# A decoder trunk in which the first MLP product is also made by seven block products, with partial sums copied from bank to bank

## The chip, the cores and the metric

The kernel runs on one core of one Trainium2 chip. Its engines are TensorE (PE, with its weight loads shown as PEld), VectorE (DVE), ScalarE (ACT), GpSimd (POOL) and SyncE (SP), which issues the loads. The metric is the device time in microseconds, as the median of several runs; one further execution was profiled.

## The reference

The reference computes four residual layers over 512 positions of width 1024, all in float32. Each mixer layer is followed by a squared-ReLU MLP with a hidden width of 4096:

```
for layer in range(2):
    h = rmsnorm(x, mix_norm_g[layer])
    x = x + (even_mixer(h) if layer % 2 == 0 else odd_mixer(h))
    h = rmsnorm(x, mlp_norm_g[layer])
    x = x + square(relu(h @ w1[layer])) @ w2[layer]
```

The even mixer is a gated position-mixing MLP beside stick-breaking attention; the odd mixer is a chunked mLSTM. Each ends with an output projection that is added to x.

## The kernel before

Everything stays on the chip: the residual `xs` is held with features on partitions (8 tiles of 128 features x 512 positions), and only weights stream in. Each operand of a float32 product is written as a high part in fp32r and a remainder (`hi`, `lo`), and a product is three matmuls: hi x hi, hi x lo, lo x hi (`mm3`, L289 to L292). So each weight tile of 128 x 1024 is split when it has landed (`w_split`, L185): ScalarE writes the high part (L189), VectorE the remainder (L190; POOL does it for the indices in `POOL_LO`). `stream` (L199) makes these units in order; `w_take` asks for them `LA = 6` units ahead; `NSPL = 5` pairs of split tiles are there. Raw tiles land in two buffers `wr` or, in the second MLP product, in `NRAW = 7` buffers `wq`.

The RMS norm isn't applied to x but folded: the gain goes into the split of x (`split_scaled`, L281), and the reciprocal root, a row over positions (`rrow`), is multiplied in when the hidden layer leaves PSUM (L725).

**At the entry of an MLP** the output projection `w_out` (L321) makes one residual tile after another (L327), and `enter` (L330) splits each of them into `xhi`, `xlo` (L282, L283) and sums its squares (L335 to L339, the sums mostly on POOL).

**The MLP** (`mlp`, L620) goes through the 4096 hidden features in `NG = 4` groups of 1024. A group has two products:

- *The first product* runs over 8 feature tiles. Each is one PSUM bank with 8 x 3 matmuls of 512 columns. VectorE takes it out with relu and the norm (L725), ScalarE squares it (L726).
- *The second product* (`second`, L658) is a 2 x 2 block product done with seven block products in place of eight (the scheme of Strassen and Winograd). Its left blocks are sums of weight blocks: `stream` makes four such sums on VectorE for each set of four weight tiles (`w_sum`, L193 to L196). Its right blocks are sums of hidden blocks: `operands` (L628) makes them from four hidden blocks in each half `q` (splits at L636 and L640, differences at L644 and L654). For each half `s` of the output columns, seven block products of 24 matmuls of 256 columns go into four banks (L674 to L676), and VectorE adds the banks to the residual and to an accumulator `accm` (L686), which is added to the residual in the last group.

PSUM has eight banks, handed out by tag: A 2, B 3, C 2, O 1. The order of the instructions on each engine isn't that of the program text: a planner simulates the program with a cost model, and each engine takes the first instruction in program order that is ready in that simulation. On the chip each engine then runs its own instructions strictly in the planned order, waiting on semaphores. Loads are issued by SP in the same way.

## Time and profile before

| | |
|---|---|
| three runs | 1139.30, 1137.31, 1139.07 us (median 1139.07) |
| the profiled execution | 1138.17 us, its span 1136.4 us |
| granted TensorE clock | 0.994 |
| busy: PE, PEld, DVE, ACT, POOL | 1105.9, 959.9, 825.9, 523.9, 163.9 us |
| loads and stores | 105.18 MB, 93 GB/s on average |

The time is that of the whole launch; the span reaches from the first to the last instruction. A busy PE includes matmuls that overlap: the distance between two starts says how fast they go. Line numbers (L290) are those of the kernel before.

### The profile page before, as it was taken

The page shows a single profiled execution, that of the slowest core. Times are in us where ns is not written, and L with a number is a line of the kernel's source. Part 1 is how long each engine was busy: PE and PEld are TensorE (multiplying, and loading weights), DVE is VectorE, ACT ScalarE, POOL GpSimd, SP SyncE. Part 2 cuts the span into 40 slices and gives each one's busy share as a digit, 9 for nine tenths or more (in the row PEclk, how much of TensorE's full clock was granted, in tenths as well). Part 3 has the DMA queues.
Part 4 walks back from the last instruction along what each step waited for, and adds up shares of the span by engine and source line. Part 5 has one row for each costly group of instructions (what it writes and reads, how often), then busy time and mean ns, then how long its engine had stood idle before and what let it go on. Part 6 is the DMA issues. An engine that isn't in the chain of part 4 may idle for free.

```text
span 1136.4 us, 15912 instructions
## 1 busy us (share of the span) xinstructions
PE 1105.9 (97%) x6372; PEld 959.9 (84%) x6372; DVE 825.9 (73%) x1135; ACT 523.9 (46%) x800; POOL 163.9 (14%) x154
## 2 busy tenths in 40 slices
PE   7899989999999999999999999999999999999998
PEld 5788767878988988988988888887899899899898
DVE  7753599468957957857977677679887677677685
ACT  5343577445435435435555444435543444444441
POOL 7316564540000000000030010003100000000000
PEclk9899999999999999999999999999999999999999
DMA  7222310242241241251042203204324224224121
GB/s 231 92 75 76 105 43 1 74 169 91 94 133 71 97 138 64 93 149 56 20 130 77 93 20 112 93 25 155 118 74 140 83 74 147 76 75 149 37 84 65
DMA packets 34506, 105.18 MB, mean 93 GB/s; under 512 B 3712, under 2 KB 10112, under 8 KB 34432
## 3 DMA queue, kind: packets, MB, share of 16 engines
q1 hardware_dynamic: 34432, 104.17, 28.4%
q8 instruction: 50, 0.82, 0.3%
q14 instruction: 24, 0.20, 0.1%
HBM read 102.06 MB, written 2.10 MB: 92 GB/s over the span
## 4 chain that ended last, share of the span: by engine, by line
PE 79%; DVE 13%; ACT 2%; issue 2%; POOL 2%; DMA 2%; SPq 0%; DVEq 0%; ACTq 0%; POOLq 0%
PE psA L292 10%; PE psA L290 10%; PE psA L291 10%; PE psB L676 7%; PE psB L674 7%; PE psB L675 7%; PE psC L291 5%; PE psC L292 5%; PE psC L290 5%; DVE m L537 2%; DVE wl L190 2%; PE psO L290 2%; PE psO L291 2%; PE psO L292 2%; DVE xlo L283 1%
## 5 line engine op out<-in xcount | busy, mean ns | idle before, releaser
L189 ACT ACTIVATE wh<-wr 128x1024 fp32r<-128x1024 f32 (+1 forms) x124 | 131.3, 1061 | 173.3 <-DMA wr<-wall 53.1
L190 DVE TENSOR_TENSOR wl<-wr,wh 128x1024 fp32r<-128x1024 f32 (+1 forms) x108 | 136.6, 1271 | 84.4 <-ACT wh L189 54.2
L189 ACT ACTIVATE wh<-wq_s 128x1024 fp32r<-128x1024 f32 x64 | 67.2, 1060 | 125.3 <-PE psC L291 57.8
L291 PE MATMUL psA<-xlo,wh 128*128 128x512 f32 x292 | 115.2, 394 | 0.0
L292 PE MATMUL psA<-xhi,wl 128*128 128x512 f32 x288 | 114.1, 396 | 0.5 <-DVE wl L190 0.5
L290 PE MATMUL psA<-xhi,wh 128*128 128x512 f32 x288 | 112.6, 392 | 1.1 <-DVE xres L327 1.1
L291 PE MATMUL psC<-xlo,wh 128*128 128x512 f32 x256 | 102.1, 399 | 0.0
L292 PE MATMUL psC<-xhi,wl 128*128 128x512 f32 x256 | 102.0, 399 | 0.0
L290 PE MATMUL psC<-xhi,wh 128*128 128x512 f32 x256 | 101.2, 395 | 0.0
L292 PE MATMUL psA<-wh,xlo 128*128 128x512 f32 (+2 forms) x232 | 87.7, 380 | 4.0 <-DVE xlo L283 2.2
L290 PE MATMUL psA<-wh,xhi 128*128 128x512 f32 (+2 forms) x232 | 88.4, 383 | 1.8 <-ACT wh L189 1.7
L189 ACT ACTIVATE wh<-wq 128x1024 fp32r<-128x1024 f32 x48 | 50.9, 1060 | 85.2 <-PE psB L675 35.1
L291 PE MATMUL psA<-wl,xhi 128*128 128x512 f32 (+2 forms) x232 | 87.7, 379 | 1.1 <-DVE wl L190 1.1
L190 DVE TENSOR_TENSOR wl<-wq_s,wh 128x1024 fp32r<-128x1024 f32 x64 | 77.5, 1219 | 3.5 <-ACT wh L189 2.5
L339 POOL TENSOR_TENSOR ssq<-ssq,sq 128x512 f32<-128x512 f32 x18 | 28.8, 1600 | 351.8 <-ACT sq L338 351.8
L725 DVE SCALAR_TENSOR_TENSOR r<-psC,rrow 128x512 f32<-128x512 f32 x32 | 22.1, 690 | 60.8 <-PE psC L292 60.8
L290 PEld LDWEIGHTS psA<-xhi,wh 128*128 128x128 f32 x288 | 54.7, 190 | 13.8 <-ACT sq L338 1.5
L291 PEld LDWEIGHTS psA<-xlo,wh 128*128 128x128 f32 x292 | 54.9, 188 | 12.2
L686 DVE TENSOR_TENSOR xres<-xres,psB 128x512 f32<-128x512 f32 x80 | 53.9, 681 | 15.4 <-PE psB L676 14.8
L292 PEld LDWEIGHTS psA<-xhi,wl 128*128 128x128 f32 x288 | 54.1, 188 | 12.2 <-DVE wl L190 0.8
L190 DVE TENSOR_TENSOR wl<-wq,wh 128x1024 fp32r<-128x1024 f32 x48 | 58.6, 1221 | 2.6 <-ACT wh L189 2.3
L290 PEld LDWEIGHTS psC<-xhi,wh 128*128 128x128 f32 x256 | 48.9, 191 | 11.1
(396 smaller groups left out, 3147.4 us busy)
## 6 DMA issues: line engine op xcount, KB each, us to landing
wr<-wall SPq DMA_DIRECT2D x122, 512.0 KB, 3.5
wq<-wall SPq DMA_DIRECT2D x64, 512.0 KB, 3.9
out<-xres SPq DMA_DIRECT2D x16, 128.0 KB, 1.8
wr<-wv SPq DMA_DIRECT2D x2, 528.0 KB, 3.5
xres<-xT SPq DMA_DIRECT2D x4, 256.0 KB, 5.7
xres<-xT SPq DMA_DIRECT2D x2, 512.0 KB, 8.6
lngb<-lngb SPq DMA_DIRECT2D x1, 512.0 KB, 5.4
sgr<-sgw SPq DMA_DIRECT2D x1, 512.0 KB, 6.2
```

What stands on the lines that cost most here:

```text
L189: act.activation(hi[:, :n], raw, AF.Copy)
L190: (gp if i in POOL_LO else dve).tensor_tensor(lo[:, :n], raw, f(hi[:, :n]), op=ALU.subtract)
L290: pe.matmul(out, lhsT=lh, rhs=rh, start=first, stop=False)
L291: pe.matmul(out, lhsT=lh, rhs=rl, start=False, stop=False)
L292: pe.matmul(out, lhsT=ll, rhs=rh, start=False, stop=last)
L339: (dve if i == KT - 1 else gp).tensor_tensor(ssq, ssq, j, op=ALU.add)
L537: dve.tensor_tensor_scan(m[:, ::-1], m[:, ::-1], ones.to_broadcast([P, n]), 1.0, op0=ALU.mult, op1=ALU.mult)
L674: pe.matmul(o, lhsT=lh, rhs=rh, start=first, stop=False, skip_group_check=True)
L675: pe.matmul(o, lhsT=lh, rhs=rl, start=False, stop=False, skip_group_check=True)
L676: pe.matmul(o, lhsT=ll, rhs=rh, start=False, stop=fin, skip_group_check=True)
L686: add = lambda dst, b, op=ALU.add: dve.tensor_tensor(dst, dst, b, op=op)
L725: dve.scalar_tensor_tensor(r, b, 0.0, rb[0], op0=ALU.max, op1=ALU.mult)
```

## The change

The first product is also made by seven block products. Its blocks are the four quarters of x (features 0 to 511 and 512 to 1023, positions 0 to 255 and 256 to 511) and those of the weights of a group. Hidden features are now made in two quarters `q` of seven products each, with 256 columns in a matmul.

The same function `product` serves both products. A bank is no longer added up on VectorE into an accumulator: after a11, ScalarE copies the bank, negated, into a second one, a12 goes on in the first, s2 in the second; after s2 ScalarE copies the second into a third, where n3 and a22 go on. So that matmuls add to what ScalarE wrote, an identity product is made into these two banks once at the start of each MLP. In the first product ScalarE also copies n1's bank to SBUF.

Both products read weights in sets of four tiles. Of the four sums of a set, VectorE makes two (`c`, and `b21` in place), and two are made by loads that add to what stands in the buffer (`w_acc`, issued by POOL). So b12 and b22 are each loaded twice. The raw buffers `wq` are 5 for 7.

At the entry the operands of the first product are made: the projection's tiles come in the order 0, 4, 1, 5, 2, 6, 3, 7, and for each pair ScalarE scales, VectorE makes one difference and three more, and seven blocks are split. The relu and square follow each block as it is finished, and the hidden blocks' sums are made from them as before. Pools are placed and opened at other points: the weights' and the sums' pools lie on the right side and are opened before the entry.

```diff
+            b11 = w_load(i, True)
+            w_split(b11, i)
+            yield
+            b = w_load(i + 1, True)
+            w_acc(b, i + 2)
+            b21 = w_load(i + 3, True)
+            w_split(b21, i)
+            yield
+            c = wpool.tile([P, 1056], F32, name=f"wc{i}", tag="wr", bufs=2)[:, :1024]
+            dve.tensor_tensor(c, b, b11, op=ALU.add)
+            w_split(c, i)
+            yield
+            dve.tensor_tensor(b21, c, b21, op=ALU.add)
+            w_acc(b11, i + 1)
+            w_split(b11, i)
+            yield
+            w_split(b, i)
+            yield
+            w_split(w_load(i + 2), i)
+            yield
+            w_split(b21, i)
...
+    def w_acc(t, i):
+        gp.dma_start(out=t, in_=wall[i if i < V0 else i - 2], accum_op=ALU.add)
...
+    def operands_of(ep, kept):
+        def operand(norm, d):
+            g, k = pc(f"g{norm}", d), d % 4
+            if d < 4:
+                t = ep.tile([P, 3, H], F32, name=f"xa{norm}_{d}", tag="xa", bufs=2)
+                act.activation(t[:, 1:], xs[:, d, :].rearrange("p (e t) -> p e t", e=2), AF.Copy, scale=g)
+                dve.tensor_tensor(t[:, 0], t[:, 1], t[:, 2], op=ALU.subtract)
+                split(e1[0][:, k, 0:2], e1[1][:, k, 0:2], t[:, 0:2])
+                kept[k] = t
+            else:
+                x = ep.tile([P, 2, H], F32, name=f"xb{norm}_{d}", tag="xb", bufs=1)
+                act.activation(x, xs[:, d, :].rearrange("p (e t) -> p e t", e=2), AF.Copy, scale=g)
+                split(e1[0][:, k, 2:4], e1[1][:, k, 2:4], x)
+                t = ep.tile([P, 3, H], F32, name=f"xc{norm}_{d}", tag="xc", bufs=1)
+                dve.tensor_tensor(t[:, 0], kept[k][:, 2], x[:, 1], op=ALU.subtract)
+                dve.tensor_tensor(t[:, 1], kept[k][:, 1], t[:, 0], op=ALU.subtract)
+                dve.tensor_tensor(t[:, 2], x[:, 0], t[:, 1], op=ALU.subtract)
+                split(e2[0][0][:, k], e2[0][1][:, k], t)
...
+            for tag in "CB":
+                pe.matmul(bank(tag, 0), lhsT=identb, rhs=identb.unsqueeze(1).to_broadcast([P, 4, P]), start=True, stop=True)
+            def product(ops, copy=None):
+                ws = dict(zip(PROD, w_take(7)))
...
+                ba, bd, bx, bc = bank("A"), bank("C", 0), bank("B", 0), bank("O")
+                prod("a11", ba, True, False)
+                act.activation(bd, ba, AF.Copy, scale=-1.0)
+                prod("a12", ba, False, True)
+                yield 0, 0, two(ba), None, None
+                prod("s2", bd, False, False)
+                act.activation(bx, bd, AF.Copy, scale=-1.0)
+                prod("n1", bc, True, True)
+                prod("n3", bx, False, False)
+                pc5 = two(bc)
+                if copy is not None:
+                    act.activation(copy, pc5, AF.Copy)
+                    pc5 = copy
+                yield 1, 1, pc5, two(bx), ALU.subtract
+                prod("n4", bd, False, True)
+                yield 0, 1, pc5, two(bd), ALU.add
+                prod("a22", bx, False, True)
+                yield 1, 0, two(bx), None, None
+            def first(q, ops):
...
+                for tb, fb, b, b2, op in product(xop, tmp("p", "ad", AD)):
+                    t = h[tb, fb] = tmp(f"h{tb}{fb}", "h", HB)
+                    if b2 is not None:
+                        dve.tensor_tensor(t, b, b2, op=op)
+                        b = t
+                    rv = rb[0][:, tb * H:(tb + 1) * H].unsqueeze(1).to_broadcast([P, 2, H])
+                    dve.scalar_tensor_tensor(t, b, 0.0, rv, op0=ALU.max, op1=ALU.mult)
+                    act.activation(t, t, AF.Square)
+                    if (tb, fb) != (1, 0):
+                        put(f"a{tb + 1}{fb + 1}", t)
+                n1 = diff("n1", h[1, 0], h[1, 1])
+                s2 = tmp("s2", "ad", AD)
+                dve.tensor_tensor(s2, h[0, 0], n1, op=ALU.subtract)
+                put("s2", s2)
+                diff("n3", h[0, 0], h[1, 0])
+                diff("n4", h[0, 1], s2)
             def second(g, ops):
                 for s in range(2):
+                    for tb, nb, b, b2, op in product(ops):
+                        x = blk(nb, tb, s)
+                        dve.tensor_tensor(x, x, b, op=ALU.add)
+                        if b2 is not None:
+                            dve.tensor_tensor(x, x, b2, op=op)
...
-        r = enter(w_out(w_take(2), y_of(3), "AAO"), 3, ssq)
+        with tc.tile_pool(name="xe", bufs=1, side="right") as ep:
+            r = enter(w_out(w_take(2), y_of(3), "AABB", HALVES), 3, ssq, operands_of(ep, {}))
```

221 lines of the change are left out of this document (87 added, 134 removed).

## The prediction

> **What bounds the kernel now.** I read the page's busy times first, then the windows over the MLP stages, then the chain of waits, then the two places where a new MLP begins.
>
> ```profile
> span 1136.4 us, 15912 instructions
> PE 1105.9 (97%) x6372; PEld 959.9 (84%) x6372; DVE 825.9 (73%) x1135; ACT 523.9 (46%) x800; POOL 163.9 (14%) x154
> PE 79%; DVE 13%; ACT 2%; issue 2%; POOL 2%; DMA 2%; SPq 0%; DVEq 0%; ACTq 0%; POOLq 0%
> ```
> ```profile
> 221.30:246.00 24.70, 22.83 (x102) 17.96 (x101) 20.67 (x22) 15.96 (x22) 13.89 (x9) 1.00 0.29 97
> 781.00:806.00 25.00, 23.67 (x104) 18.23 (x103) 24.92 (x27) 14.14 (x20) 10.45 (x8) 1.00 0.50 168
> ```
> ```profile
> 560.00:600.00 40.00, 37.73 (x311) 36.62 (x311) 30.61 (x39) 24.53 (x36) 11.73 (x16) 1.00 0.30 94
> ...
> 860.00:960.00 100.00, 100.00 (x658) 91.57 (x657) 76.36 (x90) 40.98 (x49) 0.00 (x0) 1.00 0.35 115
> 960.00:1060.00 100.00, 100.00 (x609) 89.41 (x608) 70.21 (x84) 41.65 (x51) 0.00 (x0) 1.00 0.34 106
> ```
>
> After the window come its length and the busy time of PE, PEld, DVE, ACT and POOL. Inside an MLP (860 to 1060) PE has no gap at all, at a granted clock of 1.00: what is taken from PE there is taken from the time, as long as the others keep up. VectorE is next, with 70 to 76 us in 100. At the two entries, where the output projection hands the residual to an MLP (221 to 246, 781 to 806), VectorE is nearly full already, 20.67 us in 24.70 and 24.92 in 25.00, and PE stays busy there only because it can start on the first product one input tile at a time.
>
> **The matmul saving.** PE starts in one layer group of MLP 0: first wide matmul of a stretch, first narrow one, first wide one of the next group.
>
> ```profile
> 410.50 0.39 PE L290 MATMUL psC<-xhi,wh 128*128 128x512 f32 x1
> ...
> 449.36 0.28 PE L674 MATMUL psB<-a11h,wh 128*128 128x256 f32 x1
> ```
> ```profile
> 494.89 0.39 PE L290 MATMUL psC<-xhi,wh 128*128 128x512 f32 x1
> ```
>
> From 410.50 to 449.36 PE issues seven feature tiles of 24 wide matmuls, 168: 38.86 / 168 = 0.2313 us each. From 449.36 to 494.89 it issues the 336 narrow ones of the second product (2 halves x 7 products x 24) and one wide tile of 24: (45.53 - 24 x 0.2313) / 336 = 0.1190 us. The first product is 192 wide now, 44.4 us, and becomes 2 quarters x 7 x 24 = 336 narrow, 40.0 us. That is 4.4 us in a group and **35.4 us in eight groups** (4 in each of 2 MLPs). A narrow matmul might have been held up by its weight load; the second product shows that it isn't, as its 0.119 us hold both.
>
> **VectorE's load in a group.** Durations of rows overlap by a start-up; the cost in a queue is the distance between starts:
>
> ```profile
> 376.00 0.68 DVE L686 TENSOR_TENSOR xres<-xres,psB 128x512 f32<-128x512 f32 x1
> 376.60 1.22 DVE L190 TENSOR_TENSOR wl<-wq,wh 128x1024 fp32r<-128x1024 f32 x1
> 377.74 0.69 DVE L640 TENSOR_TENSOR n4l<-n,n4h 128x512 fp32r<-128x512 f32 x1
> 378.34 1.22 DVE L196 TENSOR_TENSOR wq_s<-wq_s,wq 128x1024 f32<-128x1024 f32 x1
> ```
>
> So 0.60 us for 512 columns and 1.14 us for 1024. Now: 8 + 14 weight remainders and 8 weight sums (30 x 1.14 = 34.2), 8 relu steps, 22 operand steps, 14 residual adds (44 x 0.60 = 26.4): 60.6 us in 84.4. After: 28 remainders and 2 sums for each of 4 sets (36 x 1.14 = 41.0; the other two sums of a set go to the loads), in each quarter 4 relu steps, 2 subtractions out of a bank and 11 operand steps (34 x 0.60 = 20.4), 12 residual adds (7.2): 68.6 us in 80.0. It fits over the group. It doesn't fit over the first product alone: there 18 x 1.14 + 20.4 = 40.9 us stand against 40.0 of PE. What carries it over is the lead: five pairs of split weights (NSPL) let VectorE be up to five remainders, 5.7 us, ahead. I take no loss in the six groups that follow another group; the bound on the other side is the first rival below.
>
> ScalarE has room: 28 weight splits, 2 x (3 bank copies, 4 squares, 7 splits) and 2 x 2 bank copies are 28 x 1.06 + 32 x 0.63 = 49.8 us in 80.
>
> ```profile
> L189 ACT ACTIVATE wh<-wq_s 128x1024 fp32r<-128x1024 f32 x27 | 28.3, 1060 | 55.5 <-PE psC L291 28.2 <-PE psO L675 16.0 <-PE psB L675 7.2
> ...
> L726 ACT ACTIVATE h<-r 128x512 f32<-128x512 f32 x31 | 19.4, 625 | 6.3 <-DVE r L725 6.2
> ```
>
> **The copy between banks.** Each product begins with a11, then ScalarE copies the bank (negated) to a second one, and only then may a12 go on in the first: PE ends its last matmul 0.28 - 0.12 = 0.16 us after it could start another, the copy is as long as the 512-column row above, 0.63, and two hand-offs add about 0.03 each (the relu step started at 337.33, where the last matmul of its bank ended, 336.90 + 0.40): 0.85 us. This copy is free where n1, which goes to a bank of its own, is there to fill it: the trace shows that the order is planned so (n4 of one group stands between two wide matmuls at 494.54 and 494.66, in the midst of the next group's first tile). n1 is 24 x 0.119 = 2.86 us, enough for this gap and for the second copy after s2. It isn't there at the step from the first to the second product of a group, since its operand needs the last hidden block, which PE finished just one product earlier. I take one open gap in each group, **8 x 0.85 = 6.8 us**; bounds 0 and all four in a group, 27.
>
> ```profile
> 336.90 0.40 PE L292 MATMUL psA<-xhi,wl 128*128 128x512 f32 x1
> ```
> ```profile
> 337.33 0.69 DVE L725 SCALAR_TENSOR_TENSOR r<-psA,rrow 128x512 f32<-128x512 f32 x1 [1.42 <-PE psA L292]
> 494.54 0.28 PE L676 MATMUL psB<-n4h,wl 128*128 128x256 f32 x1
> 494.66 0.39 PE L292 MATMUL psA<-xhi,wl 128*128 128x512 f32 x1
> ```
>
> **The two entries.** Here a gain is given back. Now a residual tile needs one remainder on VectorE; after, a pair of tiles needs a difference (256 columns), two remainders of 512, three differences of 256 in a row and a remainder of 768.
>
> ```profile
> 204.69 0.42 DVE L287 TENSOR_TENSOR atl<-psC,ath 128x256 fp32r<-128x256 f32 x1
> ```
>
> With 0.34 us for 256 columns (0.42 less the same 0.08 overlap) and 0.87 for 768 (between 0.60 and 1.14), a pair costs 4 x 0.34 + 2 x 0.60 + 0.87 = 3.43 us against 2 x 0.66 now; four pairs +8.4 us. What counts for PE is when the last tile that a11 needs is split:
>
> ```profile
> L283 DVE SCALAR_TENSOR_TENSOR xlo<-xres,par,xhi 128x512 fp32r<-128x512 f32 x8 | 10.5, 1367 | 0.0
> ```
> ```profile
> 235.23 2.44 DVE L283 SCALAR_TENSOR_TENSOR xlo<-xres,par,xhi 128x512 fp32r<-128x512 f32 x2
> 796.30 2.44 DVE L283 SCALAR_TENSOR_TENSOR xlo<-xres,par,xhi 128x512 fp32r<-128x512 f32 x2
> ```
> ```profile
> 230.57 0.40 PE L290 MATMUL psA<-xhi,wh 128*128 128x512 f32 x1
> 235.36 0.51 PE L292 MATMUL psA<-xhi,wl 128*128 128x512 f32 x1 [0.46 <-DVE wl L190]
> 244.00 1.02 PE L266 MATMUL psC<-onesd,ssq 128*128 128x1 f32 x8 [1.41 <-DVE ssq L339]
> 789.89 0.40 PE L292 MATMUL psA<-yoh,wl 128*128 128x512 f32 x1
> 791.39 0.47 PE L290 MATMUL psA<-xhi,wh 128*128 128x512 f32 x1 [1.11 <-DVE xres L327]
> ```
>
> At the even entry the last remainder ends at 237.67. All but the last pair's second half (2.5 us) of the 8.4 comes before a11's last input: 243.6. Nine of a11's matmuls (1.07 us) can run ahead, so PE stands as if it had begun at 242.5, where now it begins at 230.57 and loses 0.46 + 1.41: **10.1 us lost**. At the odd entry 798.74 + 5.9 - 1.07 = 803.6 against PE's being free at 790.12, where now it loses 1.27: **12.2 us lost**. Bounds for both together: 5 if splits of weights now in front of them move behind, 36 if the first product behind each also runs at VectorE's pace (7 us more each, by rival 1 without a lead).
>
> The first set of MLP 0 has an index in POOL_LO, and in the new loop all seven remainders take that index: seven go to POOL, at
>
> ```profile
> L190 POOL TENSOR_TENSOR wl<-wr,wh 128x1024 fp32r<-128x1024 f32 x16 | 38.7, 2428 | 9.0 <-ACT wh L189 8.9
> L339 POOL TENSOR_TENSOR ssq<-ssq,sq 128x512 f32<-128x512 f32 x18 | 28.8, 1600 | 351.8 <-ACT sq L338 351.8
> ```
>
> 17.0 us. That takes 7 x 1.14 = 8.0 us off VectorE, but VectorE's remainders beside POOL's sums at the entry took 1367 ns against 690 alone (377.74 above): 8 x 0.68 = 5.4 us lost beside six sums of 1600 ns on POOL, 9.6 us, so 17.0 us would cost 9.6. I take nothing; bounds -8 and +9.6. The Trainium skill, "SBUF — State Buffer", section "Who interferes with whom", states this as a rule: a VectorE instruction with two SBUF inputs contends with a GpSimd instruction that reads SBUF. By that rule the offload is worth nothing, as the row says; without it the sum would be 8 us lower.
>
> **What else moves.** The last group of an MLP makes 12 residual adds for 20 now (8 x 0.60 = 4.8 us), where PE idles 2.3 us between 560 and 600; I take **-2**. The cleared accumulator on POOL stood beside PE's work and gives nothing. The pools' new places and the order of the projection's tiles only decide when loads may start.
>
> The two sums made by loads: b12 += b22 and b11 += b12, issued by POOL, whose queue in the MLP holds nothing else. No accumulating load is in this trace. The nearest rows:
>
> ```profile
> wr<-wall SPq DMA_DIRECT2D x122, 512.0 KB, 3.5
> wq<-wall SPq DMA_DIRECT2D x64, 512.0 KB, 3.9
> ```
> ```profile
> q1 hardware_dynamic: 34432, 104.17, 28.4%
> ```
>
> Loads rise by 64 x 0.52 MB, to some 38% of the queues' time. The sum b12 + b22 is made a set ahead and hidden. b11 + b12 is not: it may start when b11's remainder and the sum c are done, and n1's split waits for it, at the head of ScalarE's queue, with the bank copies behind it. With five pairs b11's remainder is done about 9.1 us before a11 starts, and n1's split may start 2.9 us before: 6.2 us for the load. Bounds: 3.5 us (a plain load, hidden) and 7.0 (read and add one after the other); I take the first end's side, hidden, because nothing but the add is new. By the Trainium skill, "DMA: Bandwidth & Descriptors", section "Anatomy of one DMA — SWDGE (gpsimd) path", a load on this path takes 2.0 us and its bytes at 436 GB/s, an estimate of 3.2 us, which would also be hidden; no run here shows it.
>
> **Sum:** -35.4 + 10.1 + 12.2 + 6.8 - 2 = -8.3 us. The profiled execution took 1138.17 us (span 1136.4), so 1129.9; the median of the runs lies 0.9 above it: **1131 us**.
>
> **Rivals.** (1) *VectorE becomes the bound of the first product*, slower. For: 40.9 us against 40.0, and VectorE now idles much in front of the relu steps, since the order of its queue is fixed:
>
> ```profile
> L725 DVE SCALAR_TENSOR_TENSOR r<-psC,rrow 128x512 f32<-128x512 f32 x4 | 2.8, 691 | 9.3 <-PE psC L292 9.3
> L725 DVE SCALAR_TENSOR_TENSOR r<-psA,rrow 128x512 f32<-128x512 f32 x4 | 2.8, 690 | 2.9 <-PE psA L292 2.9
> ```
>
> These 12.2 us are one group's. If half stays and half the lead is used up, the first product takes 40.9 + 6.1 - 2.9 = 44.1 us, 4.1 over PE, in six groups 24.6: **1155 us**. It decides from 1.4 us a group. Against: the second product needs only 27.7 us of VectorE in 40.0 and can refill the lead. (2) *The accumulating load is late*, slower: 7.0 us against 6.2, 0.8 us in each of 32 sets, 26 us: **1156 us**; it decides from 0.26 us a set. Against: slots may be free earlier than I reckon. (3) *The entries stay hidden*, faster: 5 us for both and the gaps filled, 1139.07 - 35.4 + 5 - 2 = **1107 us**. For: VectorE waits for PE before the even entry, and work may be moved there; against: 24.92 of 25.00 at the odd one.
>
> ```profile
> 221.35 1.29 DVE L327 TENSOR_TENSOR xres<-psA,xres 128x512 f32<-128x512 f32 x2 [9.55 <-PE psA L292]
> ```
>
> (4) *The change doesn't do what it says*: the planned order finds something else, all gains are eaten, about **1139 us**.
>
> **Chances.** Forecast 0.40 (its own range 1118 to 1142), (1) 0.20, (2) 0.10, (3) 0.22, (4) 0.08. A measurement of this kernel can tell about 0.2% (2.3 us) from no change. Of the forecast's 0.40, 0.33 is faster, 0.03 the same, 0.04 slower; (3) is faster throughout; of (1) and (2) 0.27 is slower, 0.01 the same, 0.02 faster; of (4) 0.04, 0.02, 0.02. Faster 0.61, same 0.06, slower 0.33. The range, 1105 to 1155, reaches into (3) and (1) and leaves 0.2 out.
>
> **What will show it.** Right: PE in the MLP in narrow matmuls 0.119 us apart and groups of 80 to 82 us; a PE gap of 8 to 15 us at each entry, released by VectorE's or ScalarE's work on the new sums; gaps of about 0.85 us released by ScalarE's bank copy, once a group; VectorE at 85% in the MLP. Wrong: gaps in the first product released by VectorE's remainders in every group (1); ScalarE's split idle for an accumulating load (2); no gap at the entries (3); groups near 84 us.

## The result and the profile after

The changed kernel is slower: 1222.09 us (median of 4 runs, 1219.65 to 1227.29) against 1138.19 us for the kernel before (median of 4, 1134.69 to 1139.30). The ratio is 1.0749, with a 95% interval of 1.0701 to 1.0796. The forecast was 1131 us, with a range of 1105 to 1155: the sign was wrong, and the time lies far outside the range. The profiled execution took 1219.65 us.

The head of the page after, with its busy times, the clock in 40 slices, POOL's DMA queue (packets, MB, share of 16 engines' span) and the shares of the chain of waits:

```profile
span 1217.9 us, 18697 instructions
PE 1104.1 (91%) x7528; PEld 1004.7 (82%) x7528; DVE 911.5 (75%) x1222; ACT 627.9 (52%) x954; POOL 223.5 (18%) x221
PEclk8999999869999999999999999997899999999999
q0 software_dynamic: 9216, 33.56, 15.6%
PE 41%; DMA 24%; DVE 22%; ACT 6%; issue 5%; POOL 3%; SPq 1%; POOLq 0%; ACTq 0%; DVEq 0%
```

Before, the chain was 79% PE and 2% DMA; now PE has 41% and DMA 24%. Apart from the first slice the clock drops at the two entries (slices 8 and 9, and 28 and 29 of the 40). The windows over the two entries and two times 100 us of the second MLP (length, busy time of PE, PEld, DVE, ACT and POOL, clock, DMA share, GB/s), first the kernel before at its even entry, then the changed kernel:

```profile
200.00:260.00 60.00, 58.13 (x255) 46.72 (x254) 33.96 (x41) 29.63 (x42) 28.18 (x15) 0.97 0.39 132
```
```profile
200.00:260.00 60.00, 40.72 (x174) 31.98 (x172) 41.25 (x46) 29.80 (x45) 35.72 (x20) 0.82 0.37 105
800.00:860.00 60.00, 49.15 (x224) 39.95 (x223) 52.71 (x90) 31.49 (x59) 13.39 (x12) 0.82 0.17 45
860.00:960.00 100.00, 92.17 (x744) 89.50 (x744) 74.57 (x86) 51.26 (x67) 7.80 (x9) 0.99 0.53 137
960.00:1060.00 100.00, 92.84 (x763) 90.45 (x761) 77.84 (x90) 49.69 (x65) 8.80 (x10) 1.00 0.55 137
```

Two things show at once. At the even entry PE is busy for 40.72 of 60 us, where it was busy for 58.13. And inside the MLP, where PE had no gap, it has 7 to 8 us of gaps in 100, while VectorE is hardly fuller than before (74.57 and 77.84 against 76.36 and 70.21). The chain of waits inside the MLP says what PE waits for, in the end (start, length, what). Line numbers from here on are those of the changed kernel: L197 is ScalarE's split, L198 VectorE's remainder, L203 the adding load.

```profile
864.61 1.24 DVE wl L198
865.86 4.26 DMA wq<-wall
870.16 0.59 issue
870.77 0.64 POOL wq L203
871.41 7.40 DMA wq<-wall
878.89 1.07 ACT wh L197
879.99 1.23 DVE wl L198
...
887.65 4.22 DMA wq<-wall
...
893.46 7.40 DMA wq<-wall
900.94 1.07 ACT wh L197
```

This is one turn in a set of weights, and it comes again 22 us later. A remainder of VectorE sets a raw buffer free (865.86). Only then the plain load of the next set's b12 begins (4.26 us). When it has landed, POOL issues the two adding loads, back to back, the next set's b12 + b22 and this set's b11 + b12. The first lands 5.3 us after its issue. The second, issued 0.64 us behind it in the same queue, takes 7.40 us, and ScalarE has stood idle for it, in front of the split of n1's weights. So the loop is raw buffer, load, adding load, split, remainder, raw buffer. The loads of the MLP by who issues them, with the median from issue to landing:

```profile
wq<-wall SPq DMA_DIRECT2D x96, 512.0 KB, 3.6
wr<-wall SPq DMA_DIRECT2D x90, 512.0 KB, 4.0
wq<-wall POOLq DMA_DIRECT2D x64, 512.0 KB, 5.6
```

The 5.6 us mix two kinds. By the landing times in the trace, 34 of the 64 adding loads were issued when the one before had landed, and took 5.4 us at the median; the other 30 were issued while the one before was still under way, and took 7.25.

**A measure for the stages.** A set is the 168 narrow matmuls of seven products; at 0.119 us each that is 20.0 us. An MLP has four groups of four sets: two of the first product (q0, q1), two of the second (s0, s1). From the starts of its matmuls, the time of each set of the changed kernel is, in us:

| | group 1: q0 q1 s0 s1 | group 2 | group 3 | group 4 | sum |
|---|---|---|---|---|---|
| MLP 0 | 49.0 24.9 23.8 20.0 | 21.1 24.9 24.0 20.2 | 21.1 23.1 24.0 20.4 | 21.3 23.2 23.9 23.6 | 388.3 |
| MLP 1 | 40.8 23.1 24.0 22.3 | 21.2 23.1 24.4 20.2 | 21.0 23.7 24.1 20.3 | 20.9 23.5 24.1 20.8 | 377.6 |

Both MLPs take 765.9 us, where 32 dense sets would take 640. The rest of the launch takes 1219.65 - 765.9 = 453.8 us. Nearly all the experiments below have 453 to 460 us for that rest, too, so they are compared by their MLPs. The kernel before, from the first wide matmul of an MLP to its last narrow one, takes 346.6 and 340.9 us, 687.5 for its two. Nearly all the experiments are single runs, each good to some 8 us (the changed kernel's four took 1219.65 to 1227.29, the kernel before 1134 to 1140 beside these runs). They are set against the profiled execution of the changed kernel, the fastest of its four; the sets agree better than that.

### The profile page after: what moved, and what is told of

The parts are those of the page before. It is cut to its first block, busy times and chain, and to the rows that moved or that the text cites. A ratio compares the mean times of both kernels' runs of the same rounds, so it can differ in the third digit from the quotient of the medians.

```text
span 1217.9 us, 18697 instructions
## 1 busy us (share of the span) xinstructions
PE 1104.1 (91%) x7528; PEld 1004.7 (82%) x7528; DVE 911.5 (75%) x1222; ACT 627.9 (52%) x954; POOL 223.5 (18%) x221
## 3 DMA queue, kind: packets, MB, share of 16 engines
q0 software_dynamic: 9216, 33.56, 15.6%
## 4 chain that ended last, share of the span: by engine, by line
PE 41%; DMA 24%; DVE 22%; ACT 6%; issue 5%; POOL 3%; SPq 1%; POOLq 0%; ACTq 0%; DVEq 0%
DMA wq<-wall 22%; DVE wl L198 7%; PE psA L298 5%; PE psA L300 5%; PE psA L299 5%; ACT wh L197 3%; PE psB L697 2%; PE psO L300 2%; PE psO L298 2%; PE psA L698 2%; PE psO L299 2%; PE psA L697 2%; DVE m L588 2%; PE psA L699 2%; PE psB L698 2%
## 5 line engine op out<-in xcount | busy, mean ns | idle before, releaser
L197 ACT ACTIVATE wh<-wq 128x1024 fp32r<-128x1024 f32 x160 | 168.2, 1056 | 220.3 <-DMA wq<-wall 97.6
L198 DVE TENSOR_TENSOR wl<-wq,wh 128x1024 fp32r<-128x1024 f32 x155 | 190.6, 1231 | 72.3 <-ACT wh L197 72.1
L203 POOL DMA_DIRECT2D wq<-wall x64 | 56.6, 964 | 610.0 <-DMA wq<-wall 282.3
L197 ACT ACTIVATE wh<-wr 128x1024 fp32r<-128x1024 f32 (+1 forms) x92 | 97.2, 1058 | 57.1 <-DMA wr<-wall 32.7
L198 DVE TENSOR_TENSOR wl<-wr,wh 128x1024 fp32r<-128x1024 f32 (+1 forms) x77 | 97.4, 1269 | 36.3 <-ACT wh L197 33.4
L698 PE MATMUL psA<-xlo,wh 128*128 128x256 f32 x256 | 76.9, 300 | 10.4 <-DVE xlo L295 10.3
L697 PE MATMUL psA<-xhi,wh 128*128 128x256 f32 x256 | 77.0, 301 | 4.4 <-ACT psC L704 4.2
L697 PE MATMUL psB<-xhi,wh 128*128 128x256 f32 x256 | 73.0, 285 | 4.6 <-ACT psB L708 4.6
L699 PE MATMUL psA<-xhi,wl 128*128 128x256 f32 x256 | 75.6, 295 | 0.0
L699 PE MATMUL psB<-xhi,wl 128*128 128x256 f32 x256 | 72.1, 282 | 0.0
L698 PE MATMUL psB<-xlo,wh 128*128 128x256 f32 x256 | 72.0, 281 | 0.0
L697 PE MATMUL psC<-e2h,wh 128*128 128x256 f32 x256 | 71.3, 279 | 0.0
L698 PE MATMUL psC<-e2l,wh 128*128 128x256 f32 x256 | 71.1, 278 | 0.0
L197 ACT ACTIVATE wh<-wc 128x1024 fp32r<-128x1024 f32 x32 | 33.9, 1060 | 38.5 <-PE psB L698 30.7
```

What stands on the lines that cost most here:

```text
L197: act.activation(hi[:, :n], raw, AF.Copy)
L198: (gp if i in POOL_LO else dve).tensor_tensor(lo[:, :n], raw, f(hi[:, :n]), op=ALU.subtract)
L203: gp.dma_start(out=t, in_=wall[i if i < V0 else i - 2], accum_op=ALU.add)
L697: pe.matmul(o, lhsT=lh, rhs=rh, start=first, stop=False, skip_group_check=True)
L698: pe.matmul(o, lhsT=lh, rhs=rl, start=False, stop=False, skip_group_check=True)
L699: pe.matmul(o, lhsT=ll, rhs=rh, start=False, stop=fin, skip_group_check=True)
```

## The experiments

All the kernels are the changed one with the edit shown, if nothing else is said. Where an instruction is left out, the planner makes a new order, which can cost or give some us by itself.

### The adding loads

In the first kernel the two adding loads of a set are left out; in the second they are plain loads into the same buffers. In both the sums b12 + b22 and b11 + b12 are missing from the result.

```diff
 e1_no_acc
-        gp.dma_start(out=t, in_=wall[i if i < V0 else i - 2], accum_op=ALU.add)
+        pass
 e2_plain_load
-        gp.dma_start(out=t, in_=wall[i if i < V0 else i - 2], accum_op=ALU.add)
+        gp.dma_start(out=t, in_=wall[i if i < V0 else i - 2])
```

> The changed kernel without its 64 accumulating loads: the two weight sums of a set that they make are left out (b12 and b11 go on as they landed); splits, VectorE's two sums, copies and matmuls all stay. The changed kernel's profiled execution took 1219.65 us: 81.5 more than before = -35.4 (matmuls) + some 44 (PE's standstill at the two entries, less what it was before) + some 73 over eight groups. Theory A (the wait for accumulating loads, with the raw buffers behind them, makes the 73): most of it goes, 1150 to 1165. Rival B (VectorE, with 68.6 us of work in a group of 80 and an order that is fixed, makes it): no more than 15 us go, 1205 or more. Rival C (the bank copies on ScalarE make it): as B.

> The changed kernel with the same 64 loads from POOL's queue as plain loads, without the add: they overwrite (so two sums of a set are left out), and every wait, buffer and byte stays. If it is the add that makes these loads slow (5.6 us from issue to landing against 3.6 for the others): landing falls to about 4 and the time by 20 to 50 us. If it is the chain itself (slot free, load, issue from POOL, load again, sum, split): less than 15 us go, 1205 to 1220.

Without the loads: 1189.07 us, between what the two theories expected; this kernel has a new planned order, and its s0 sets take 24.3 us where plain loads leave 23.2, so its time isn't the price of the loads alone. With plain loads: 1175.49 us, and this kernel has the same planned order as the changed one on every engine, the same bytes and the same number of loads. So 1219.65 - 1175.49 = **44.2 us are the price of the add alone**, 46.3 in the MLPs (719.6 for 765.9). Its page and its loads:

```profile
q0 software_dynamic: 9216, 33.56, 8.4%
```
```profile
wq<-wall POOLq DMA_DIRECT2D x64, 512.0 KB, 4.2
```

For the same 33.56 MB the queue's share is 8.4% where it was 15.6%, and a load lands in 4.2 us where it took 5.6 (3.8 for 5.4 when the one before had landed, 4.5 for 7.25 when it was still under way). The difference of the medians is 1.4 us, and 64 of them would be 90 us if they all counted; half of it does. By position in a group (mean of groups 2 to 4, both MLPs; s1 without the last group), the sets take:

| | q0 | q1 | s0 | s1 |
|---|---|---|---|---|
| changed kernel | 21.1 | 23.6 | 24.1 | 20.3 |
| plain loads | 19.7 | 21.0 | 23.2 | 20.0 |

The adds cost some 5.2 us in a group, most of it in the first product, where VectorE has most to do by the prediction's count.

**The kernel before with adding loads** in its second product, with its seven raw buffers:

```diff
 e4_before_acc (the kernel before)
-                b12 = w_load(i + 1, True)
-                b22 = w_load(i + 2, True)
-                b = w_sum(b12, b22)
+                b = w_load(i + 1, True)
+                w_acc(b, i + 2)
...
-                w_split(w_sum(b11, b12), i)
+                w_acc(b11, i + 1)
+                w_split(b11, i)
```

> The kernel before with one part of the change alone: in the second product b12+b22 and b11+b12 are made by accumulating loads from POOL in place of VectorE (7 raw buffers as before, 16 sets in place of 32). Theory A in its strong form (the load's own time is what costs): 16 sets x 2.3 us = 35 us, 1165 to 1180. Weak form (the load costs only where raw buffers are few, 5 in the change): 1137 to 1145, since here 7 buffers serve sets that are needed half as often.

1148.23 us against 1140.1 for the kernel before on the same chip: 8.1 us for 16 sets, 0.5 us a set, though VectorE is spared 32 sums. That lies between the two forms of the theory, just above the weak one, and it is a difference of two single runs. An adding load lands in 5.4 us here, and each was issued when the one before had landed:

```profile
wq<-wall POOLq DMA_DIRECT2D x32, 512.0 KB, 5.4
```

So the operation is as slow where everything else is as before. With two raw buffers more, and a set needed half as often, it costs a third as much in a set (46.3 / 32 = 1.4 us).

**A sixth raw buffer**, for b21 of every second set (room is made by four hidden buffers for five, and by smaller constants):

```diff
 e5_six_raw
-            b21 = w_load(i + 3, True)
+            b21 = w_load(i + 3, True, (i - m) % 8 == 4)
...
+            raw = mpool[0].tile([P, 1024], F32, name=f"wx{i}", tag="wx", bufs=1)
```

> The changed kernel with a sixth raw buffer (b21 of every second set has one of its own; one hidden-block buffer fewer makes the room), so that two sets can be in the buffers at once: b12 of the next set can land, and take its accumulating load, while the present set is in use. e2 showed that 44 us go when the same loads don't add, in the same order of every engine. Theory A1 (the add is late because the loads start late, when a buffer comes free): 15 to 40 us go, 1180 to 1205. Rival A2 (the add is late because of its own length, wherever it starts: the planned order leaves it about 4 us and it takes 5.6): less than 10 us go, 1210 to 1222.

1193.33 us, 26 us less, with adding loads that land no sooner (6.1 us). The sets q0 and q1 come down to 20.1 and 21.1, nearly as with plain loads, and the MLPs take 737.7 us, 28 of the 46.3 less. So more than half of what the adds cost comes from the lack of raw buffers: the chain of loads starts too late to hide.

**All four sums on VectorE**, with b22 loaded once:

```diff
 e6_dve_sums
-            w_acc(b, i + 2)
+            b22 = w_load(i + 2)
+            dve.tensor_tensor(b, b, b22, op=ALU.add)
...
-            w_acc(b11, i + 1)
+            dve.tensor_tensor(b11, c, b22, op=ALU.subtract)
```

> One part of the change undone: no accumulating loads, all four sums of a set on VectorE (b += b22, c = b + b11, b21 += c, b11 = c - b22), b22 landing once in the two other raw buffers. VectorE's load rises from 68.6 to 77.7 us in a group of 80. If VectorE has the room: about what e2 took, 1165 to 1185. If VectorE is the bound (rival B): 5 us and more in a group on top of e2, 1215 and more.

1231.40 us, 12 more than with adding loads. In the MLP VectorE then has 87.71 us in 100:

```profile
960.00:1060.00 100.00, 94.17 (x766) 92.99 (x765) 87.71 (x99) 52.81 (x68) 0.00 (x0) 0.97 0.31 102
```

The first product isn't what gets longer: in the later groups q0 takes 19.7 and q1 22.5 us, less than in the changed kernel, but s0 takes 27.0 for 24.1, and the rest of the launch 462 for 454. So all four sums on VectorE are no cheaper than the adding loads. That VectorE couldn't have made them in time isn't shown apart, since b22 here also holds one of the two buffers that the sum c uses.

**The order of the adding loads.** POOL's planned queue has, for three sets in four, the next set's first adding load ahead of this set's second one, which is n1's. This edit queues the second one ahead:

```diff
 e18_add_order
+        with (ExitStack() if b11 or last[0] is None else tc.issue_after(last[0])):
+            ins = gp.dma_start(out=t, in_=wall[i if i < V0 else i - 2], accum_op=ALU.add)
+        if b11:
+            last[0] = ins.ins
```

> The whole computation. In the changed kernel POOL's queue has, for three sets in four, the next set's first adding load (b12 + b22) ahead of this set's second one (b11 + b12, n1's weights); the first waits for a plain load into a raw buffer that comes free late. Here the second one is queued ahead. Theory (n1's weights are late because their load stands behind the other one in POOL's queue): they come some us earlier in each set, and half or more of the 46 us of the adding loads is had back, 1180 to 1200. Rival (the raw buffers set the pace, and what one load gains the other loses, since the next set's sum b then comes later): 1210 to 1235.

1232.66 us, 13 more: the rival holds. What POOL waits for is another thing now, a remainder of VectorE in place of a load that has to land. First the changed kernel, then this one:

```profile
POOL wq L203 <- DMA wq<-wall: 282.3, 20, 24.4
POOL wq L203 <- DVE wl L198: 172.2, 10, 24.2
```
```profile
POOL wq L206 <- DVE wl L198: 545.7, 28, 27.0
POOL wq L206 <- DMA wq<-wall: 63.0, 11, 24.3
```

q0 and q1 take 20.8 and 23.4 us, a little less than before, but s0 takes 26.3 for 24.1. So this other order doesn't help. It fits the waits that what n1 gains, the next set's b loses, for want of time between a raw buffer's release and its next use.

### The step to the second product

With plain loads s0 still takes 23.2 us. PE's rows in one such set of that kernel, at its two gaps, and ScalarE's at the same time:

```profile
961.32 0.28 PE L699 MATMUL psO<-n1h,wl 128*128 128x256 f32 x1
963.03 0.38 PE L697 MATMUL psA<-a12h,wh 128*128 128x256 f32 x1 [1.42 <-ACT psC L704]
...
971.07 0.28 PE L698 MATMUL psA<-a11l,wh 128*128 128x256 f32 x1
972.63 0.38 PE L697 MATMUL psB<-n3h,wh 128*128 128x256 f32 x1 [1.28 <-ACT psB L708]
```
```profile
959.97 1.06 ACT L197 ACTIVATE wh<-wq 128x1024 fp32r<-128x1024 f32 x1 [1.79 <-PE psB L698]
960.93 0.62 ACT L744 ACTIVATE h<-h 128x512 f32<-128x512 f32 x1
961.45 1.04 ACT L197 ACTIVATE wh<-wr 128x1024 fp32r<-128x1024 f32 x1
962.40 0.58 ACT L704 ACTIVATE psC<-psA 128x512 f32<-128x512 f32 x1
...
964.99 0.64 ACT L294 ACTIVATE n1h<-n 128x512 fp32r<-128x512 f32 x1 [0.94 <-DVE n L733]
...
971.03 1.06 ACT L197 ACTIVATE wh<-wq 128x1024 fp32r<-128x1024 f32 x1 [0.94 <-PE psC L698]
971.99 0.58 ACT L708 ACTIVATE psB<-psC 128x512 f32<-128x512 f32 x1
```

Both gaps end with a bank copy (L704, L708), and the copy stands in ScalarE's queue behind a split of weights that had to wait for PE (at 959.97 and 971.03). From start to start PE loses 1.71 - 0.12 and 1.56 - 0.12, 3.0 us together. Three kernels ask whether that is the copies, VectorE's load, or the operands that come late. All three have plain loads (two sums left out). In addition, the first has no copies from bank to bank: s2 and n3 begin their banks anew, so the partial sums are not carried on. The copy of n1's bank to SBUF stays.

```diff
 e7_no_copies
-                act.activation(bd, ba, AF.Copy, scale=-1.0)
...
-                prod("s2", bd, False, False)
-                act.activation(bx, bd, AF.Copy, scale=-1.0)
+                prod("s2", bd, True, False)
...
-                prod("n3", bx, False, False)
+                prod("n3", bx, True, False)
```

> e2 (plain loads) without ScalarE's two bank copies in each product: the second and third bank begin with their own first matmul, so the sums lack the products that the copies carry over. Against e2's 1175.49. If PE's wait for the copies makes the 29 us that e2 leaves in the groups: 1145 to 1157. If it is hidden but for one gap in each group, as predicted (6.8 us): 1165 to 1172. If nothing: within 4 us.

1186.25 us, 11 more, which none of the three expectations had. In a new planned order q1 takes 19.6 us for 21.0 and s0 26.7 for 23.2. Where the copies stood, PE now waits (860 to 1170 us) for the copy of n1's bank to SBUF (L711), for the subtraction ahead of relu (L738) and for an operand (L294):

```profile
PE psO L697 <- ACT p L711: 6.8, 3, 5.1
PE psB L697 <- DVE h L738: 4.8, 3, 1.6
PE psA L697 <- ACT a12h L294: 3.8, 3, 1.3
```

So the copies account for some of q1's gap, but leaving them out doesn't close the gap in s0; as the order is new, it doesn't show more than that. The next two take nearly the same off VectorE in a first product, 4.6 and 4.8 us, but only the second shortens the way from the last hidden block to the operands. The first leaves out both weight sums of VectorE as well; the second leaves out the four differences of hidden blocks and splits the blocks themselves.

```diff
 e11_no_sums
-            dve.tensor_tensor(c, b, b11, op=ALU.add)
-            w_split(c, i)
+            w_split(b, i)
...
-            dve.tensor_tensor(b21, c, b21, op=ALU.add)
 e12_no_chain
-                    dve.tensor_tensor(d, a, b, op=ALU.subtract)
-                    put(n, d)
-                    return d
+                    put(n, a)
+                    return a
...
-                dve.tensor_tensor(s2, h[0, 0], n1, op=ALU.subtract)
+                s2 = h[0, 0]
```

> Left out: the adding in the loads, and both weight sums that VectorE makes in a set (b12 and b21 as loaded are split in their place). This takes 2 x 1.14 us of VectorE from each set, 36 to 34 operations of the weights being left. Theory (VectorE is the bound of the first product, 40.9 us against 40.0, and its lateness shows in the first set of the second product, 23.2 us for 20): at 36.3 against 40.0 the second and third sets of a group come down to 20 to 21 us, 8 x 3 to 4 us less, about 1148. Rival (the chain of hidden operands behind the last block, not VectorE's load): the third set stays at 23, 1168 to 1176.

> Left out: the adding in the loads, and the four differences of hidden blocks in each quarter; the blocks themselves are split in their place, so that no operand waits for another. This takes 8 x 0.6 = 4.8 us off VectorE in a first product, as much as the two weight sums are in its two sets (4.6). Theory of VectorE's load: as much as without the weight sums, about 1148. Rival (the chain n1, s2, n4 behind the last block sets it): third set 20 to 21 for 23.2, 1150 too, while the run without weight sums gains nothing; if neither gains, the cause is in neither.

Without the sums s0 takes 22.6 us for 23.2, and 1164.57 us in all: 10 less in the MLPs, about half of it in s0. The first set of MLP 0 shrinks by 4.8 us, that of MLP 1 grows by 2.8. Without the differences s0 takes **20.0 us in every one of the six later groups**, and 1149.70 us in all; the MLPs take 693.1 for 719.6, 26.5 less. With as much taken off VectorE in both, it is the chain n1, s2, n4 behind the last hidden block that makes the gap, and hardly VectorE's load.

The chain can also be gone around: a22 needs only a block that is there early. In this kernel it is made third in s0, in a bank of its own.

```diff
 e15_a22_early
-                ws = dict(zip(PROD, w_take(7)))
+                ws = dict(zip(("a11", "a12", "a22", "s2", "n1", "n3", "n4") if early else PROD, w_take(7)))
...
+                if early:
+                    by = bank("B", 2)
+                    prod("a22", by, True, True)
                 prod("s2", bd, False, False)
```

> The whole computation. In the first half of each second product, a22 (whose operand is there early) is made third, in a bank of its own, ahead of s2, n1, n3, n4, which wait for the chain of hidden operands; its weights come third too; VectorE adds one bank more to the residual. Theory (the chain leaves PE idle for 3.2 us in a group): a22's 2.9 us fill the gap, 8 x 2.5 to 3 us less than 1222, about 1199; n1's weights, made by the adding load, get 2.9 us more, which can give some us more. Rival (the adding loads decide there too, and PE only waits one product later): 1215 to 1225.

1209.79 us, 10 less than the profiled execution of the changed kernel, between the theory's 1199 and the rival's range. s0 comes down from 24.1 to 20.0 us, so the gap is filled as the theory says, 4.1 us in each group. But s1 behind it goes from 20.3 to 22.0, and in the first groups to 27.3 and 26.8, and the MLPs gain only 15.6 of 33. That the adding loads take the rest back would fit, as ScalarE waits for loads as long as in the changed kernel (32.1 against 31.7 us from 870 to 1070); it wasn't tried with plain loads.

### The entries

The first set of each MLP takes 49.0 and 40.8 us. PE's planned order and VectorE's queue at the even entry, in the changed kernel (the first fence PE, the second VectorE, the third POOL):

```profile
237.60 0.58 PE L697 MATMUL psO<-e2h,wh 128*128 128x256 f32 x1 [1.49 <-ACT e2h L294]
245.57 0.58 PE L698 MATMUL psO<-e2l,wh 128*128 128x256 f32 x1 [7.39 <-DVE e2l L295]
```
```profile
239.09 3.42 DVE L228 TENSOR_TENSOR wq<-wc,wq 128x1024 f32<-128x1024 f32 x1
242.43 3.09 DVE L295 TENSOR_TENSOR e2l<-xc,e2h 128x768 fp32r<-128x768 f32 x1
```
```profile
238.84 5.86 POOL L198 TENSOR_TENSOR wl<-wq,wh 128x1024 fp32r<-128x1024 f32 x2
```

A weight sum that takes 1.22 us elsewhere takes 3.42 beside POOL, and the remainder of 768 columns 3.09; PE stands for both behind one matmul of n1, whose place in its order was planned without that. Afterwards PE is slow too: most of its matmuls from 253 to 265 us start 0.213 us apart, in the slice where the clock shows 6 tenths (244 to 274 us).

```diff
 e3_pool_28
-    POOL_LO = range(14, 30)
+    POOL_LO = range(14, 28)
```

> The changed kernel with POOL_LO ending at 28: the seven remainders of MLP 0's first set go to VectorE, as all others. Theory D (POOL's remainders and VectorE's work on two SBUF inputs hold each other up at the even entry: e2l 3.09 us there against 0.96 later): PE's standstill between 230 and 265 shrinks by 8 to 15 us, 1205 to 1212. Rival (the entry is set by ScalarE and the planned order): within 4 us of 1219.65. The prediction had put this at nothing, between 8 lower and 9.6 higher.

Here VectorE makes the first set's remainders. 1217.8 us, 1.9 less: the first set gains 5.3 us (43.7), and the others, under the adding loads, give most of it back. The next kernel leaves out the three differences at the entry and the split of 768 columns (their place is filled by ScalarE with a constant):

```diff
 e8_no_e2
-                dve.tensor_tensor(t[:, 0], kept[k][:, 2], x[:, 1], op=ALU.subtract)
-                dve.tensor_tensor(t[:, 1], kept[k][:, 1], t[:, 0], op=ALU.subtract)
-                dve.tensor_tensor(t[:, 2], x[:, 0], t[:, 1], op=ALU.subtract)
-                split(e2[0][0][:, k], e2[0][1][:, k], t)
```

> The changed kernel without the second half of the operands at the two entries: the three differences and the split of 768 columns for each pair of tiles are left out, and the three operands hold a constant. Against 1219.65. Theory E (VectorE's and ScalarE's work on these sums, held up by POOL, makes the entries' 44 us): 20 to 35 us go, 1185 to 1200. Rival (the entries stand still because a11 needs whole tiles and PE's clock falls): less than 10 us go.

1229.04 us. The first sets shrink to 33.4 and 33.6, but MLP 0 starts 11 us later, behind the filling, and the next sets grow to 28.2 and 27.5. This test was spoilt by its own filling and by the adding loads. So it was made again with plain loads and without filling (three products read blocks of x that are there); beside it POOL was kept out of the entry, and then both together.

```diff
 e9_entry_plain (with e8's lines out)
-                    ("n1", e2[0], 0), ("s2", e2[0], 1), ("n4", e2[0], 2))}
+                    ("n1", e1, 0), ("s2", e1, 1), ("n4", e1, 2))}
 e10_pool_out (with e3's line)
-                (dve if i == KT - 1 else gp).tensor_tensor(ssq, ssq, j, op=ALU.add)
+                dve.tensor_tensor(ssq, ssq, j, op=ALU.add)
```

> Left out: the adding in the loads (plain loads, as in the run of 1175.49 us) and, at both entries, the three differences and the split of 768 columns of each pair; the three products that used them read three of the blocks of x that are there already, so nothing has to be filled. The time goes by the two first sets, 45.6 and 38.4 us in that run for 20. Theory (the entry's work on VectorE holds the first sets up, and what took over in the run that only left this work out was the adding loads): first sets near 32 each and nothing behind them longer, so 18 to 22 us less, about 1155. Rival (behind the entry's work the weights are as late anyway): at most 5 us less, 1170 to 1177.

> Plain loads again (the two sums left out, 1175.49 us). POOL is kept out of the entry: the first set's remainders and the sums of squares are made by VectorE. Theory (VectorE's steps of 3 us at the entry are long because POOL reads beside them): steps of 1024 columns are 1.2 us and of 768 columns 1.0 us again; VectorE gets 7 x 1.14 + 6 x 0.6 = 11.6 us more at the first entry and 3.6 at the second, against some 15 us of stretching at each; both first sets shorter, together by 5 to 15 us, 1160 to 1170. Rival (VectorE is full there whatever its partner does): first sets as long or longer, 1175 to 1185.

> Plain loads (the two sums left out), and both edits to the entry together: the differences of x and their split left out (in that run alone the two first sets took 37.5 and 31.2 us for 45.6 and 38.4), and POOL kept out of the entry (alone 40.1 and 35.0). Theory (one cause, VectorE's queue at the entry, lengthened by the new operands and stretched by POOL beside it): the two edits add up, first sets near 32 and 28, what follows hardly longer, some 10 us less than either alone, about 1157. Rival (the weights of the first set come late anyway): first sets as in the better one alone, 36 and 31, about 1165.

| plain loads and | time, us | first sets | both MLPs |
|---|---|---|---|
| nothing else | 1175.49 | 45.6, 38.4 | 719.6 |
| no differences of x (e9) | 1165.38 | 37.5, 31.2 | 712.7 |
| POOL out of the entry (e10) | 1170.53 | 40.1, 35.0 | 715.4 |
| both (e13) | 1156.39 | 33.4, 29.5 | 701.9 |

In the first sets the edits nearly add up: 15.3 and 8.9 us alone, 21.1 together. So these 21 us are the new operands in VectorE's queue and the stretching beside POOL, and late weights don't hold the first sets where the better edit alone left them. Of the 44.0 us that the first sets take over 40 with plain loads, 22.9 stay. In them PE at the even entry mostly waits for the blocks of x themselves (3.2 us for VectorE's remainders, 2.2 for ScalarE's high parts, of 7.2); what else holds them was not tried. That POOL is what stretches VectorE's steps shows in VectorE's groups, first the changed kernel and then the one with POOL kept out (230 to 280 us; count | busy, mean ns):

```profile
L295 DVE TENSOR_TENSOR xlo<-xb,xhi 128x512 fp32r<-128x512 f32 x4 | 6.0, 1498 | 0.0
L295 DVE TENSOR_TENSOR e2l<-xc,e2h 128x768 fp32r<-128x768 f32 x4 | 6.0, 1491 | 1.8 <-ACT e2h L294 1.8
L228 DVE TENSOR_TENSOR wq<-wc,wq 128x1024 f32<-128x1024 f32 x2 | 4.6, 2318 | 0.0
```
```profile
L295 DVE TENSOR_TENSOR e2l<-xc,e2h 128x768 fp32r<-128x768 f32 x4 | 3.8, 957 | 1.2 <-ACT e2h L294 1.2
L295 DVE TENSOR_TENSOR xlo<-xb,xhi 128x512 fp32r<-128x512 f32 x4 | 2.7, 685 | 0.0
L228 DVE TENSOR_TENSOR wq<-wc,wq 128x1024 f32<-128x1024 f32 x2 | 2.4, 1223 | 0.0
```

With plain loads and POOL where it was, the means are as in the first fence: 1500, 1491 and 2315 ns.

### Everything together

This kernel takes out all the causes named so far: plain loads, no differences of hidden blocks, none of x, POOL out of the entry. It doesn't compute the layers; it asks what is left of the time.

> All causes named so far taken out at once: plain loads (two sums left out), no differences of hidden blocks, no differences of x at the entry, POOL out of the entry. Theory (these are the whole account, and what is left is the matmul saving): both MLPs together 640 us and some 25 to 30 of entry and end, so 1149.7 less some 20: 1125 to 1132, a little below the kernel before; from second set to last every set at 20 to 21 us. Rival (a further cause is still hidden under these): over 1138.

1128.62 us, against 1136.88 for the kernel before on the same chip. Its MLPs take 674.0 us, 91.9 less than the changed kernel's 765.9. The parts, each measured by its own step, add up to nearly that: 46.3 (adds) + 26.5 (chain) + 17.7 (entries, e13 against plain loads) = 90.5. Inside the MLP PE is dense again:

```profile
860.00:960.00 100.00, 99.73 (x839) 99.50 (x838) 80.52 (x88) 54.48 (x69) 5.29 (x10) 1.00 0.49 158
960.00:1060.00 100.00, 99.78 (x838) 99.54 (x837) 83.01 (x93) 56.11 (x73) 5.30 (x10) 1.00 0.48 159
```

Of the 34.0 us that it still has over 640, 22.9 lie in the two first sets.

Two kernels join what helped: the sixth raw buffer, a22 third in s0, POOL out of the entry; the second has the order of the adding loads, too.

> The whole computation, with the three edits that helped: a sixth raw buffer for every second set (alone 26 us), a22 third in the first half of each second product, and POOL out of the entry (alone 4 us of the MLPs with plain loads). Theory: they add up, 1222 - 26 - 20 - 5 = 1171. Rival (the buffer's gain and that of a22 are one and the same, time for the adding load): 1185 to 1192. It isn't expected to come down to the kernel before.

> The whole computation: the sixth raw buffer, a22 third in the first half of each second product, POOL out of the entry (together 1186.25), and the order of the adding loads as in the run beside this one. Theory (queue order): 10 to 25 us less, 1160 to 1176, still over the kernel before. Rival (the raw buffers): 1180 to 1200.

The first took 1186.25 us, 33 less than the changed kernel and 7 less than the sixth buffer alone: 26, 10 and some 4 us don't add up, and s1 now takes 26.1 us; that the three share the adding loads' slack is the likely reason, but wasn't tried. The second took 1222.0 us (median of 4; ratio to the kernel before 1.0739, 1.0707 to 1.077), over both expectations, so the order costs 36 us there. Neither comes near the kernel before.

## Why the prediction was wrong, step by step

**The matmul saving, -35.4 us: right in size.** Narrow matmuls are 0.119 us apart in the first product as well: with plain loads q0 takes 19.7 us, and in the kernel with all causes out every set of groups 2 to 4 but the last takes 19.9 to 20.5. With all that goes wrong taken out, the kernel is 8 us faster than before, though it still carries 22.9 us at the entries.

**The adding loads, 0 us: wrong, 46.3 us, the largest error.** The step that failed is "hidden, because nothing but the add is new". The upper bound was named, 7.0 us against 6.2 of slack, and priced as rival (2) at 0.8 us a set; the cost is 1.4 us a set. An adding load with none under way ahead of it took 5.4 us, more than the plain load's 3.5 but inside the 6.2; one issued behind another took 7.25 at the median, over it, and the working had priced one load at a time. Two things in it were wrong beside that. The sum b12 + b22 was taken as "made a set ahead and hidden"; in the trace its plain load starts only when a remainder frees a raw buffer, and both adding loads stand behind it on POOL, whose queue "holds nothing else". And the change from seven raw buffers to five, for twice as many sets, was given no term; the sixth buffer gives back 26 us. By the Trainium skill, "DMA: Bandwidth & Descriptors", section "Anatomy of one DMA — SWDGE (gpsimd) path", the load was 3.2 us as an estimate; the plain load from POOL took 4.2, and the adding one 5.6.

**The bank copy, 6.8 us: right place, wrong size, 26.5 us.** The gap was put rightly where the first product goes over into the second, and "once a group". It was sized as one copy that starts at once, 0.85 us. There are two gaps of 1.6 and 1.4 us, since each copy stands in ScalarE's queue behind splits that wait. n1, which was to cover the second copy, has an operand from the chain of VectorE and ScalarE steps behind the last hidden block: in the rows shown it is split at 964.99, behind the first gap, and n1 is done before the second. Without the chain s0 takes 20.0 us. Nor was it quite once a group: in q1, too, PE waits for the second copy (0.63 us at 950.13 with plain loads).

**The entries, 10.1 + 12.2 us: right mechanism in part, little over half the size.** Counted as PE's loss from its first product matmul, the forecast's steps were 242.5 - 230.57 = 11.9 and 803.6 - 790.12 = 13.5 us. With plain loads the first sets exceed 20 us by 25.6 and 18.4. That the two sums come near to what stays with the differences and POOL out (25.4 against 22.9) is chance, as the forecast's steps were made of those differences and their splits. One step that failed is the price of VectorE's operations: 0.34, 0.60 and 0.87 us from rows where POOL was quiet, although rows from beside POOL stood in the same part, 2.44 us for two remainders and 1367 ns for one; they were used only where remainders move to POOL. The rule weighed there, of the Trainium skill, "SBUF — State Buffer", section "Who interferes with whom", agrees with the runs: 1491 ns beside POOL and 957 without it. The forecast also let PE run ahead by nine matmuls; the planned order had matmuls of n1 between a11's, and one of them waited 7.39 us. And it had no term for the matmuls that come 0.213 us apart behind the gaps; with plain loads those are some 5 us of the 44.

**The first set's remainders on POOL, 0 us: right in number.** Undone, they change the time by 1.9 us, within the noise of a single run. That is partly luck: the first set alone gets 5.3 us shorter without them, and the sets behind it give most of that back.

**VectorE as the bound of the first product, rival (1): no.** VectorE has 75 to 78% in the MLP after, not the 85% forecast, as PE is slower; and taking 4.6 us off it in each first product gave 10 us in eight groups. With all four weight sums on it q0 and q1 got no longer than in the changed kernel, and the loss lay in s0. Rival (2), the late adding load, came nearest to what happened, with a chance of 0.10. Rival (3), hidden entries, didn't hold: the first sets lose 44.0 us even with plain loads.

**The account.** The forecast's sum for the profiled execution was 1129.9 us, the execution took 1219.65: 89.8 us. The adding loads are 46.3 of it, the chain 26.5 - 6.8 = 19.7, the entries 25.6 + 18.4 - 25.4 = 18.6, together 84.6. The other 5 us were not followed up, nor was the -2 us for the last group.

What stays open: why an adding load keeps its queue busy twice as long, and what makes the 22.9 us that the first sets keep. And the chain was shown by leaving out its differences; which of its steps, VectorE's difference or ScalarE's split behind it, is worth most was not tried apart.

## What to carry to other kernels

A transfer that does arithmetic has to be measured before it is called hidden, and its start is set by the whole loop (buffer free, load, add, split, buffer free), so a cut in the number of buffers needs a term of its own in the sum. Where a bank copy or another short step sits on an engine with an ordered queue, its price isn't its length but the wait of what stands ahead of it; look for work that is ready early, as a22 was, to put in the gap. Take durations for a crowded place from rows of that place, and when several causes share the same slack, expect single repairs to be given back by the next one until all are out.

## What the runs showed of the hardware that was not expected

A load that adds to what is in SBUF took 5.6 us at the median for 512 KB against 4.2 for a plain one from the same queue and 3.6 from SP. Issued when the one before had landed it took 5.4 us (plain: 3.8), behind one still under way 7.25 (plain: 4.5); for the same 33.56 MB, its queue was busy 15.6% of 1217.9 us against 8.4% of 1173.7, 190 against 99 us on the mean of the 16 engines. VectorE's two-input operations took up to three times as long while POOL worked on SBUF (3.09 us for 0.96 at 768 columns, 3.42 for 1.22 at 1024).
